# Batched attention on one Trainium2 core: the last K chunk of the first batch turned by a DMA transpose, and V released by another transpose

## The chip, the cores and the metric

The kernel runs on one core of one Trainium2 chip. The metric is the device time of one execution in microseconds (us), on the slowest core, which here is the only one. Engines are named as in the profile: PE (TensorE, matmuls), PEld (its weight loads), DVE (VectorE), ACT (ScalarE), POOL (GpSimd) and SP (SyncE). DMAs are issued from two places: POOL's queue (q0 in the profile, `software_dynamic`), which carries the loads that also cast from f32 to f16, and SP's queue (q1, `hardware_dynamic`), which carries plain copies, the output stores and the DMA transposes. Both run on the core's 16 DMA engines.

## The reference

Eight independent batches of softmax attention, 2048 rows of 512 each, in f32:

```python
batch, seq_len, d_model = 8, 2048, 512
scores = np.matmul(q, k.transpose(0, 2, 1)) / np.sqrt(d_k)
attn_weights = special.softmax(scores, axis=-1).astype(np.float32)
return np.matmul(attn_weights, v)
```

## The kernel before

**Work and tiles.** Everything on the matrix side is f16. For each batch K and Q are needed with the 512-long axis on the partitions, so they are transposed once; V is used as loaded. A batch has 16 blocks of 128 K rows, held as four chunks of four blocks (`kops[0..3]`), and 2048 queries, held as two spans of 1024 (`qraw[0]` and `qraw[1]`), each of two chunks. Chunks are called k0 to k3, q0 to q3 and v0 to v3 here: one chunk is 512 rows, 512 KB in f16. Q chunks 0 and 1 fill span one, 2 and 3 span two.

**How products are made.** Except for the first span of the first batch, both the scores and the product with V are computed by seven half-size products instead of eight (a Winograd form). This needs sums of blocks, made on DVE: `k_sums` (L181 to L184), `q_sums` (L191 to L194), `p_sums` (L327 to L330) and `v_sums` (L208 to L211). `Group.product` (matmuls at L278) makes scores of the span that is one ahead, `Pair.product` (matmuls at L373) multiplies exponentials with V. In the steady part these two kinds alternate on PE by a table of slots.

**The start of the program.** The first span of batch 0 has nothing ahead of it, so it is computed with plain matmuls (`plain_quarter` at L240, `plain_tile` at L227) while the data arrives. This stage fills about the first 41 us, and the change lies wholly in it. Its order is written out by hand, and every engine and queue follows its own instructions in that order:

- SP first loads q0 and k0 in rows of 128 (`load_first`), in f32; they are rounded and turned on PE.
- POOL then issues the cast loads, in this order: k1 (two halves), q1, k2, k3, q2, q3 (`load`, L118). k1 and k2 go to tiles of the pool `stage`; q1, k3, q2 and q3 go to four spare parts of `vraw[1]`, which no V needs yet. That is why the profile calls these `vh<-in_q_dram` and `vh<-in_k_dram`.
- k1, q1, k2 and k3 are turned on PE by `pe_transpose`: 16 matmuls against the identity (L153) into two PSUM tiles of the tag `px`, one copied out by DVE and one by ACT (L156). k3's stands ahead of the tile (10, 1); its first use is the tile (12, 0).
- q2 and q3 are turned by SP with `dma_transpose` (L143), SBUF to SBUF, one DMA each, in this order.
- POOL then makes a one-element copy, the gate (L576), from the last element of `qraw[1]`, which q3's transpose writes. The four V loads (`load_v`, L200) stand behind it on POOL, so they are not issued before q3's transpose has landed. Behind them, on the same queue, come the first loads of batch 1.
- When the plain tiles are done, PE starts the slot loop: the second span's scores, and from slot 5 on the first product with V (`FIRST` begins with `a1`), whose eight matmuls read v0 to v3 one after another.

The transposes on SP wait for their source to be loaded; SP executes nothing else between them and the first store, at 57 us.

Of the kernel before, what the change touches and what calls it, by code (L numbers as in the profile page):

```python
# [12 lines left out]
def kernel(  # L13
# [21 lines left out]
    nc = tc.nc  # L35
# [10 lines left out]
    ND = D // P  # L46
# [3 lines left out]
    NT = QH // P  # L50
    NQT = 2 * NSP
    NJ = NKB // 2
    CH = 4
# [22 lines left out]
    def bank(name):  # L76
        t = psum[name].tile([P, 512], F32, tag=name)
        return t
# [14 lines left out]
    qraw = [const.tile([P, 2 * NT, ND, P], F16, name=f"qraw{n}") for n in range(2)]  # L93
# [40 lines left out]
    def raw_of(what, b, c):  # L134

        if what == "k":
            return kops[c][0]
        return qraw[(b * NCH + c) // 2 % 2][:, c % 2 * CH:(c % 2 + 1) * CH]

    def dma_transpose(what, b, c):  # L140
        src = staged.pop((what, b, c))
        dst = raw_of(what, b, c)
        nc.sync.dma_start_transpose(  # L143
            out=dst[:, 0:CH].rearrange("p n c r -> p (n c) r"),
            in_=src[:].rearrange("p n d -> p (n d)"),
        )

    def transposed(what, c, n, w, copy):
        src = staged[what, 0, c]
        tr = psum["px"].tile([P, 2, ND, P], F16, tag="px", name="tr")  # L150
        for m in range(w):
            for dc in range(ND):
                nc.tensor.transpose(  # L153
                    tr[:, m, dc, :], src[:, n + m, dc * P:(dc + 1) * P], ident[:]
                )
        copy(out=raw_of(what, 0, c)[:, n:n + w], in_=tr[:, 0:w])  # L156
        if n + w == CH:
            staged.pop((what, 0, c))

    def pe_transpose(what, c, n0=0, n1=CH):  # L160
        for n in range(n0, n1, 2):
            transposed(what, c, n, 2, nc.scalar.copy if n else nc.vector.tensor_copy)
# [14 lines left out]
    def k_sums(c):  # L177
        a11, a12, a21, a22 = k_blocks(c)
        _, s1, s2, s4 = kops[c]
        return [  # L180
            lambda: add(s1[:], a21, a22),  # L181
            lambda: sub(a21, a11, a21),
            lambda: sub(s2[:], s1[:], a11),
            lambda: sub(s4[:], a12, s2[:]),  # L184
        ]

    def q_sums(sp):
        b11, b12, b21, b22 = q_blocks(sp)
        t1, t2, t4 = qsum
        return [  # L190
            lambda: sub(t1[:], b12, b11),  # L191
            lambda: sub(t2[:], b22, t1[:]),
            lambda: sub(b12, b22, b12),
            lambda: sub(t4[:], b21, t2[:]),  # L194
        ]
# [23 lines left out]
    def exp(out_, in_):  # L219
        nc.scalar.activation(out=out_, in_=in_, func=EXP, scale=inv_sqrt_d)  # L220

    def plain_tile(kb, half, name):

        st = bank(name)
        c, n = divmod(kb, CH)
        for dc in range(ND):
            nc.tensor.matmul(  # L227
                st[:], kops[c][0][:, n, dc, :], qraw[0][:, half * NT:(half + 1) * NT, dc, :],
                start=(dc == 0), stop=(dc == ND - 1),
            )  # L230
        left, right = pts[0]
        exp(right[:, kb // 2, kb % 2, :] if half else left[kb % 2][:, kb // 2, :], st[:])

    def plain_quarter(j, part):

        st = bank("qx")
        w = QH // 2
        for s in range(2):
            for dc in range(ND):
                nc.tensor.matmul(  # L240
                    st[:, s * w:(s + 1) * w], kops[0][0][:, 2 * j + s, dc, :],
                    qraw[0][:, 2 * part:2 * part + 2, dc, :],
                    start=(s == 0 and dc == 0), stop=(dc == ND - 1), skip_group_check=True,
                )
        for s in range(2):
            exp(pts[0][0][s][:, j, part * w:(part + 1) * w], st[:, s * w:(s + 1) * w])
# [67 lines left out]
    def p_sums(g, which, j0=0, j1=NJ):  # L314

        left, right = pts[g // 2]
        if (g, which) not in psums:
            psums[g, which] = [
                spool.tile([P, NJ, P], F16, tag=f"s{n}", name=f"s{n}") for n in (1, 2, 4)
            ]  # L320
        s1, s2, s4 = psums[g, which]
        cols = columns(g, which)
        js = slice(j0, j1)
        a11, a21 = left[0][:, js, cols], right[:, js, 0, cols]
        a12, a22 = left[1][:, js, cols], right[:, js, 1, cols]
        return [
            lambda: add(s1[:, js], a21, a22),  # L327
            lambda: sub(s2[:, js], s1[:, js], a11),
            lambda: sub(a21, a11, a21),
            lambda: sub(s4[:, js], a12, s2[:, js]),  # L330
        ]
# [198 lines left out]
    gate = const.tile([P, 1], F32)  # L530
# [39 lines left out]
    plain_quarter(1, 0)  # L570
    pe_transpose("k", 1, 0, 2)
    plain_quarter(1, 1)
    dma_transpose("q", 0, 2)
    dma_transpose("q", 0, 3)

    nc.gpsimd.tensor_copy(out=gate[:], in_=qraw[1][:, 2 * NT - 1, ND - 1, 0:1])  # L576
    for c in range(NCH):
        load_v(0, c)

# [3 lines left out]
    for n, (kb, half) in enumerate(rest):  # L583
        if (kb, half) == (5, 0):
            pe_transpose("k", 1, 2, 4)
        if (kb, half) == (6, 0):
            pe_transpose("q", 1)
        if (kb, half) in ((6, 1), (10, 1)):
            pe_transpose("k", kb // CH + 1)
        plain_tile(kb, half, "qz" if n % 3 == 2 else "qx")  # L590
        if half and kb % CH == 3:
            background.extend(k_sums(kb // CH))
        if (kb, half) == (12, 1):
            background.extend(p_sums(0, "a", 0, NE))
        if (kb, half) == (13, 1):
            background.extend(q_sums(1))
        if background:
            background.popleft()()
# [58 lines left out]
```

The softmax here doesn't subtract the row's maximum and nothing guards it: scores larger than these inputs give would overflow.

## Time and profile before

The median of five runs is 804.93 us (804.04 to 806.69). The profiled execution is one of the five.

| What | us |
|---|---|
| Median of the five runs | 804.93 |
| The profiled execution, its own time | 806.69 |
| Its span from the first to the last instruction | 804.9 |
| PE busy in the span | 795.5 (99%) |
| ACT busy | 571.2 (71%) |
| DVE busy | 547.9 (68%) |
| q0's packets, as a share of the 16 DMA engines' span | 42.8% |
| q1's packets, the same | 38.5% |

PE is busy nearly all the time and ran at the full granted clock (0.999). Of its waits in the first 70 us, one is long: 2.1 us at L373 for a V load. Waits of PE in this stretch, by what it waited for: the V load 2.1 us, the memset of the warm-up tile 1.2, the first rows' rounding 0.8, a copy of Q 0.6 in two pieces, q1's load 0.4, and a sum for V 0.3.

### The profile page before, as it was taken

What the parts mean: (1) busy time and instruction counts of PE and PEld (TensorE: products, weight loads), DVE (VectorE), ACT (ScalarE), POOL (GpSimd) and SP (SyncE); (2) the same over time, 40 slices, a digit from 0 to 9 for tenths busy, and PEclk for the clock granted to TensorE, in tenths of its full rate; (3) what the DMA queues carried; (4) which work ended last, traced back from release to release, by engine and by line L of the source; (5) the groups of instructions that cost most, each with busy time, mean ns of one, the idle gap of its engine ahead of it and who ended that gap; (6) DMA issues with size and microseconds to landing.
All of it is one profiled execution on the core that took longest, in us unless ns stands there. A gap on an engine that the chain in (4) does not pass through costs nothing.

```text
span 804.9 us, 14513 instructions
## 1 busy us (share of the span) xinstructions
PE 795.5 (99%) x5516; PEld 535.6 (67%) x5516; DVE 547.9 (68%) x1213; ACT 571.2 (71%) x1021; POOL 71.6 (9%) x104
## 2 busy tenths in 40 slices
PE   8989999999999999999999999999999999999998
PEld 4556666666666666666666666666666666666677
DVE  3475766857678676776757677686776857668564
ACT  5757777777777777777677677677777777776752
POOL 3301100011100111010100110001100011000000
PEclk9999999999999999999999999999999999999999
DMA  9999993699938999289993999949997499711112
GB/s 207 160 201 200 201 145 93 119 209 197 146 77 151 190 178 177 61 152 197 179 145 87 162 173 189 139 92 173 170 184 120 95 208 168 155 40 41 48 46 104
DMA packets 190229, 116.32 MB, mean 145 GB/s; under 512 B 124496, under 2 KB 172880, under 8 KB 190160
## 3 DMA queue, kind: packets, MB, share of 16 engines
q0 software_dynamic: 49648, 49.29, 42.8%
q1 hardware_dynamic: 140368, 66.08, 38.5%
q8 instruction: 43, 0.70, 0.4%
q14 instruction: 26, 0.21, 0.1%
q10 hardware_dynamic: 144, 0.03, 0.0%
HBM read 100.70 MB, written 33.55 MB: 167 GB/s over the span
## 4 chain that ended last, share of the span: by engine, by line
PE 94%; DMA 5%; POOL 1%; DVE 0%; issue 0%; ACT 0%; SPq 0%; POOLq 0%
PE t L373 49%; PE t L278 45%; DMA vh<-in_q_dram 2%; DMA vh<-in_v_dram 2%; DMA first<-in_q_dram 1%; DMA qraw<-vh 1%; POOL vh L200 0%; POOL vh L118 0%; ACT o L381 0%; DVE stage L132 0%; DVE qraw L156 0%; SPq L128 0%; POOL stage L118 0%; PE tr L153 0%; PE t L240 0%
## 5 line engine op out<-in xcount | busy, mean ns | idle before, releaser
L278 PE MATMUL t<-qraw,kraw 128*128 128x512 f16 x720 | 194.7, 379 | 0.0
L381 ACT ACTIVATE o<-t,r 128x256 f32<-128x256 f32 x256 | 121.3, 474 | 100.2 <-DVE r L401 67.3
L373 PEld LDWEIGHTS <-s 128*128 128x128 f16 x1536 | 150.3, 98 | 57.0
L220 ACT ACTIVATE left<-t 128x512 f16<-128x512 f32 (+1 forms) x260 | 154.6, 596 | 41.7 <-PE t L278 37.1
L384 DVE SCALAR_TENSOR_TENSOR o<-t,r,o 128x256 f32<-128x256 f32 x192 | 92.4, 482 | 108.7 <-PE t L373 52.1
L278 PEld LDWEIGHTS <-kraw 128*128 128x128 f16 x960 | 93.9, 98 | 62.2
L373 PE MATMUL t<-vh,left 128*128 128x256 f16 x1024 | 133.0, 273 | 2.1 <-DMA vh<-in_v_dram 2.1
L278 PE MATMUL t<-qs,ks 128*128 128x512 f16 x480 | 133.1, 379 | 0.3 <-DVE vt L208 0.3
L373 PE MATMUL t<-vt,s 128*128 128x257 f16 (+1 forms) x1024 | 133.0, 273 | 0.0
L220 ACT ACTIVATE right<-cz 128x1024 f16<-128x1024 f32 x120 | 127.3, 1061 | 1.1 <-DVE cz L298 1.1
L373 PEld LDWEIGHTS <-left 128*128 128x128 f16 x1024 | 100.2, 98 | 39.6 <-issue 2.5
L373 PEld LDWEIGHTS <-right 128*128 128x128 f16 x1024 | 100.2, 98 | 38.4 <-issue 0.4
L292 ACT COPY cz<-t 128x512 f32<-128x512 f32 x120 | 70.2, 585 | 72.7 <-PE t L278 72.3
L298 DVE TENSOR_TENSOR cz<-t,cz 128x512 f32<-128x512 f32 x120 | 82.4, 687 | 51.7 <-PE t L278 51.7
L301 DVE TENSOR_TENSOR cz<-t,cz 128x512 f32<-128x512 f32 x120 | 82.7, 689 | 37.4 <-PE t L278 37.4
L278 PEld LDWEIGHTS <-ks 128*128 128x128 f16 x720 | 70.4, 98 | 47.4 <-issue 0.8
L278 PE MATMUL t<-qs,kraw 128*128 128x512 f16 x240 | 71.4, 379 | 0.0
L278 PE MATMUL t<-qraw,ks 128*128 128x512 f16 x240 | 71.4, 379 | 0.0
L288 ACT COPY t<-t 128x512 f32<-128x512 f32 x120 | 68.4, 570 | 3.3 <-PE t L278 0.6
L295 ACT COPY cz<-t 128x512 f32<-128x512 f32 x120 | 69.8, 582 | 0.2 <-PE t L278 0.2
L373 PE MATMUL t<-vt,right 128*128 128x256 f16 x512 | 67.2, 273 | 0.0
L373 PE MATMUL t<-vh,s 128*128 128x257 f16 x512 | 66.7, 273 | 0.0
(54 smaller groups left out, 577.2 us busy)
## 6 DMA issues: line engine op xcount, KB each, us to landing
out_dram<-o SPq DMA_DIRECT2D x127, 256.0 KB, 3.1
vh<-in_v_dram POOLq DMA_DIRECT2D x32, 512.0 KB, 9.8
stage<-in_k_dram POOLq DMA_DIRECT2D x29, 512.0 KB, 7.0
stage<-in_q_dram POOLq DMA_DIRECT2D x28, 512.0 KB, 8.0
vh<-in_q_dram POOLq DMA_DIRECT2D x3, 512.0 KB, 13.2
first<-in_q_dram SPq DMA_DIRECT2D x2, 256.0 KB, 3.7
first<-in_k_dram SPq DMA_DIRECT2D x2, 256.0 KB, 3.9
cz<-in_q_dram SPq DMA_DIRECT2D x2, 256.0 KB, 5.0
```

The source lines that it names most:

```text
L220: nc.scalar.activation(out=out_, in_=in_, func=EXP, scale=inv_sqrt_d)
L278: nc.tensor.matmul(dst[:], lhs[:, j, dc, :], rhs[:, :, dc, :], start=(n in (1, 5) and dc == 0), stop=(dc == 1), skip_group_check=True,)
L288: nc.scalar.copy(out=self.y[:], in_=self.x[:])
L292: nc.scalar.copy(out=self.cz[:, 1, :], in_=self.z[:])
L295: nc.scalar.copy(out=self.cz[:, 0, :], in_=self.x[:])
L298: nc.vector.tensor_add(self.cz[:, 1, :], self.x[:], self.cz[:, 1, :])
L301: nc.vector.tensor_add(self.cz[:, 0, :], self.z[:], self.cz[:, 0, :])
L373: nc.tensor.matmul(dst[:, 0:width], lhs(j), rhs(j), start=(first and j == 0), stop=(j == NJ - 1), skip_group_check=True,)
L381: nc.scalar.activation(out=out_, in_=src, func=COPY, scale=r[:])
L384: nc.vector.scalar_tensor_tensor(out=out_, in0=src, scalar=r[:], in1=out_, op0=MULT, op1=ADD)
```

## The change

k3 is no longer turned on PE. A DMA transpose for it is put on SP's queue, ahead of those of q2 and q3. The gate in front of the V loads reads the last element of the first half of `qraw[1]`, which q2's transpose writes, instead of the last of the second half, which q3's writes.

```diff
     plain_quarter(1, 0)
     pe_transpose("k", 1, 0, 2)
     plain_quarter(1, 1)
+    dma_transpose("k", 0, 3)
     dma_transpose("q", 0, 2)
     dma_transpose("q", 0, 3)
 
-    nc.gpsimd.tensor_copy(out=gate[:], in_=qraw[1][:, 2 * NT - 1, ND - 1, 0:1])
+    nc.gpsimd.tensor_copy(out=gate[:], in_=qraw[1][:, NT - 1, ND - 1, 0:1])
     for c in range(NCH):
         load_v(0, c)
...
             pe_transpose("k", 1, 2, 4)
         if (kb, half) == (6, 0):
             pe_transpose("q", 1)
-        if (kb, half) in ((6, 1), (10, 1)):
-            pe_transpose("k", kb // CH + 1)
+        if (kb, half) == (6, 1):
+            pe_transpose("k", 2)
         plain_tile(kb, half, "qz" if n % 3 == 2 else "qx")
```

On the engines: PE loses 16 transposes (L153), DVE and ACT lose one copy each (L156), SP gains one DMA transpose in front of the two it has. POOL keeps the same instructions in the same order; only what the gate reads differs. After the start of batch 0 no engine's instructions change.

## The prediction

> **What bounds the kernel now.** I read the page's chain shares first, then the chain in order of time over the first 52 us, then PE's and SP's own timelines there, then the DMA engines stretch by stretch.
>
> ```profile
> PE 94%; DMA 5%; POOL 1%; DVE 0%; issue 0%; ACT 0%; SPq 0%; POOLq 0%
> ```
>
> The end is set by PE for 94% of the span. The 5% of DMA can only be at the start, and the chain shows where (start, us, what):
>
> ```profile
> 12.01 15.09 DMA vh<-in_q_dram
> ...
> 27.11 4.38 DMA qraw<-vh
> ...
> 31.63 0.18 POOL gate L576
> ...
> 32.08 1.31 POOL vh L200 x2
> ...
> 34.28 12.68 DMA vh<-in_v_dram
> ...
> 47.00 0.38 PE t L373 x2
> ```
>
> From 12 to 47 us the end hangs on transfers: q3's load, q3's transpose (landed at 31.49), the gate, the V issues, v3's landing at 46.96. From 47 us on it is PE without a gap. So what counts is when v3 lands, or, if that comes early enough, when PE is ready for it. PE's timeline:
>
> ```profile
> 31.24 1.06 PE L153 MATMUL tr<-ident,vh 128*128 128x128 f16 x16
> ...
> 43.91 0.96 PE L373 MATMUL t<-vh,left 128*128 128x256 f16 x6
> 47.00 0.38 PE L373 MATMUL t<-vh,left 128*128 128x256 f16 x2 [2.13 <-DMA vh<-in_v_dram]
> ```
>
> k3's transposes cost PE 32.13 - 31.24 = 0.89 us until the next tile starts, 1.06 with the overlap; I take 1.0. PE then waits 2.13 us for v3. SP's queue (start, time SP spends on the issue):
>
> ```profile
> 24.53 5.21 SPq L143 DMA_TRANSPOSE qraw<-vh  x2
> 49.63 5.43 SPq L143 DMA_TRANSPOSE qraw<-stage  x1
> ...
> 155.06 4.97 SPq L143 DMA_TRANSPOSE qraw<-stage  x1
> 160.13 3.66 SPq L143 DMA_TRANSPOSE kraw<-stage  x1
> ```
>
> The issue of one transpose holds SP 2.63 and 1.41 us for q2 and q3 (the min and max of this group), but about 5 us where loads keep the DMA engines full. Last, the DMA engines (stretch, length, busy us of PE, PEld, DVE, ACT, POOL, clock, DMA share, GB/s):
>
> ```profile
> 22.00:25.00 3.00, 3.00 (x25) 1.70 (x24) 0.81 (x3) 2.20 (x4) 0.00 (x0) 1.00 1.23 204
> 25.00:27.10 2.10, 2.10 (x16) 1.08 (x14) 1.72 (x5) 1.61 (x3) 0.00 (x0) 1.00 1.05 139
> 27.10:31.20 4.10, 4.10 (x20) 1.86 (x19) 0.78 (x3) 2.99 (x5) 0.00 (x0) 1.00 1.10 216
> 31.20:35.00 3.80, 3.80 (x31) 2.21 (x30) 1.53 (x4) 2.78 (x5) 3.10 (x5) 1.00 0.36 36
> 35.00:47.00 12.00, 9.56 (x46) 4.32 (x45) 9.27 (x23) 6.89 (x12) 3.06 (x6) 1.00 1.20 190
> ```
>
> Loads alone run full at 204 GB/s; the change-over to transposes is poorer (139); transposes alone make 216; then there is a hole of 3.8 us (36 GB/s) between q3's transpose and V's full rate; then V. The hole is free room.
>
> [...] Where loads and the transpose of 49.63 meet (54 to 56 us), the packets are about equal in number, and a load's is 1 KB, a transpose's 256 bytes:
>
> ```profile
> q0 software_dynamic: 307, 0.31, 92.1%
> q1 hardware_dynamic: 299, 0.08, 29.4%
> ```
>
> Loads alone moved 0.41 MB in 2 us (51 to 53), so they fall to 76%, and a transpose gets some 40 GB/s. [...] 216 is measured here and is what I use.
>
> **The change part by part.**
>
> *PE.* 16 transposes go: -1.0 us at 31 us. PE comes to v3's matmuls at 44.87 - 1.0 = 43.9 instead of 44.87. If v3 still lands at 46.96 this only makes the wait 3.1 us instead of 2.1. DVE and ACT lose a 0.69 and a 1.01 us copy, off the path: nothing. Should v3 be on time, the floor is -1.0 - 2.1 = -3.1 us.
>
> *k3's transpose on SP.* k3 was issued on POOL at 10.54 and landed after 11.4 us, at 21.9. So the transpose issues at 21.9, where the DMA engines are full of q2 and q3 until 27.1. Its use moves to 31.1 us, so it has 9.2 us. The transpose of 49.63 took 10.5 us to land, but under loads that went on to 58.2 us (the last issued at 37.25, landing after 20.9). That of 155.06 took 9.0, until 164.1. Here the loads end at about 27, and q2's transpose before landed at 24.53 + 4.7 = 29.2. I take k3 landing by 30: no wait. If it is late by a microsecond or two, the 3.1 us of slack ahead of v3 hide it.
>
> *q2's transpose and the gate.* q2's transpose follows on SP when k3's issue is over, so it inherits the place that q3's had. Two pairs in the trace bound it. Before's pair q2, q3 took from 24.53 to 31.49, 7.0 us for both. The pair issued under loads at 155.06 and 160.13 landed second at 160.13 + 5.7 = 165.8, 10.8 us. From 21.9 that gives 28.9 to 32.7 for q2 against 31.49 for q3 before: the gate moves by -2.6 to +1.2 us. The low end has a reason against it: the engines have no free room before 25 us, so k3's packets before then only push q2's and q3's loads back. Only the poor change-over from 25 to 27.1 can be filled, worth 2.1 x (1 - 139/204) = 0.7 us. I take -0.6.
>
> *q3's transpose beside V.* It now runs after the gate: 0.52 MB / 216 GB/s = 2.4 us of the engines. If it follows q2's packets without a gap it is over about 2 us after the gate, and V's first packets were seen some 2 us after it (33.5 against 31.63) and V's full rate 3.4 us after it. So it mostly fits in the hole. The bounds are 0 and the whole 2.4 us. I take +0.6, a quarter of it, because V's first packets are then shared. q3's next reader is `q_sums` on DVE at 37.63, three microseconds later than I expect it landed; behind it on DVE stand the sums for k3, and behind those PE's products, all of which run into the V wait anyhow.
>
> *Queues.* On SP nothing but the first store (57.17) is behind the three transposes. On POOL, V and then batch 1's loads move with the gate; their transposes start at 49.63 and are first read at L191 at 87.39 us, so a microsecond is hidden. Nothing after the start is reordered.
>
> Sum: v3 lands at 46.96 - 0.6 + 0.6 = 46.96, PE's gain becomes waiting: 0.0 us. The profiled execution's own time is 806.69, of which its span is 804.9 and 1.8 lie around it; it is 1.76 above the median of the runs. As the sum is zero I set the forecast at the median, **804.9 us**. What can be told from no change is about 0.2%, 1.6 us.
>
> **The rivals.**
>
> *No change* (the forecast, 58%): 803.4 to 806.5. V's landing moves by less than 1.6 us either way. For it: the DMA engines are full from 10 to 31 us, and a third transpose adds work there that roughly eats the hole it fills.
>
> *V pays for q3's transpose* (slower, 26%): 807.3. If q3's issue is held on SP as that of 49.63 was (5.4 us), its packets are still queued when V comes to full rate. From then they take turns with V's, V drops to 76%, and v3 lands up to 2.4 us later, 804.93 + 2.4 = 807.3. It decides from the point where most of q3's 2048 packets are left 3.4 us after the gate; then the gate itself being late (+1.2) would add to it. For it: SP's 5 us issues, and that a transpose trickles as long as loads run. Against it: the three are queued before V is, and two queued transposes ran 216 GB/s without a gap.
>
> *V comes early* (faster, 16%): 802.3. If k3's packets pass between the loads and q2's pair time stays 7.0 us, the gate opens 2.6 us earlier, v3 lands near 44.4, still after PE's 43.9, and all of it is gained: 804.93 - 2.6. Against it: no free DMA room before 25 us. At the most it is -3.1.
>
> That the DMA transpose doesn't do its part is no rival: k3 has nine microseconds.
>
> **How the numbers follow.** 58, 26 and 16 in a hundred, and the chances of same, slower and faster are these, since each case lies on one side of 0.2%. The range goes from 802.4 to 807.5: it holds the forecast's own and a little over half of each of the other cases, and leaves out gains over 2.5 us and losses over 2.6.
>
> **What would show it.** In the profile after: no L153 at 31 us; k3's transpose issued near 21.9 with an issue of 2.6 to 5.4 us; the gate between 29 and 32.7; v3's landing within 1.6 of 46.96; and a PE wait at L373 of about 3 us. I am wrong if that wait is under 1.5 us (V came early), if v3 lands after 48.6 with transpose packets still among V's, or if PE waits for k3 near 31 us for so long that it sets the end.

## The result, and the profile after

The changed kernel takes 809.45 us (median of 26 runs, 805.88 to 816.0) against 805.09 us for the kernel before (47 runs, 803.69 to 810.82). The ratio is 1.0054, 95% interval 1.0042 to 1.0066: slower by 4.4 us. The profiled execution took 810.99 us, with a span of 808.8; it is 1.5 us above its median.

The chain shares of the page hardly differ from before:

```profile
PE 93%; DMA 5%; POOL 0%; DVE 0%; issue 0%; ACT 0%; SPq 0%; ACTq 0%; POOLq 0%
```

The chain in order of time (start, us, what) at the start, and a second stretch of it that the kernel before does not have:

```profile
11.40 14.42 DMA vh<-in_q_dram
...
25.84 6.40 DMA qraw<-vh
...
32.37 0.18 POOL gate L577
...
35.02 12.71 DMA vh<-in_v_dram
...
47.77 0.59 PE t L373 x2
...
70.00 0.18 SPq L143
...
70.28 10.71 DMA out_dram<-o
...
81.08 0.48 ACT o L381
```

The gate follows q2's transpose now, and comes 0.74 us later than before (32.37 against 31.63); v3 lands at 47.73 instead of 46.96. That is a fifth of the 3.9 us by which the two spans differ. The rest is in PE's own timeline (the bracket is the idle time ahead and what ended it):

```profile
43.66 0.60 PE L373 MATMUL t<-vh,left 128*128 128x256 f16 x4
45.23 0.38 PE L373 MATMUL t<-vh,left 128*128 128x256 f16 x2 [0.98 <-DMA vh<-in_v_dram]
47.77 0.59 PE L373 MATMUL t<-vh,left 128*128 128x256 f16 x2 [2.16 <-DMA vh<-in_v_dram]
48.16 1.91 PE L278 MATMUL t<-qraw,kraw 128*128 128x512 f16 x4
49.86 1.66 PE L373 MATMUL t<-vt,s 128*128 128x257 f16 x8
...
81.60 1.03 PE L373 MATMUL t<-vt,s 128*128 128x256 f16 x8 [1.18 <-ACT o L381]
```

The two groups after v3 in the kernel before:

```profile
47.22 1.02 PE L278 MATMUL t<-qraw,kraw 128*128 128x512 f16 x4
48.08 1.04 PE L373 MATMUL t<-vt,s 128*128 128x257 f16 x8
```

Two things are to be seen. After v3 the next four matmuls take 1.91 us and the eight after them 1.66; the same groups took 1.02 and 1.04 before. And at 81.60 PE waits 1.18 us for ACT, a wait that the kernel before doesn't have. The table of PE by stretches (length, busy time, granted clock, DMA share, GB/s) tells what the first is:

```profile
44.00:46.00 2.00, 0.63 (x5) 1.00 1.25 209
46.00:48.00 2.00, 0.23 (x2) 0.93 1.24 205
48.00:50.00 2.00, 2.00 (x7) 0.50 1.24 205
50.00:52.00 2.00, 2.00 (x12) 0.72 1.25 207
52.00:54.00 2.00, 2.00 (x15) 1.00 1.24 206
```

PE was busy 0.86 us of 4, and then the clock was granted at 0.50. The lost time is 2 x 0.07 + 2 x 0.50 + 2 x 0.28 = 1.7 us, that is 3.4 us at half clock.

In this trace the clock was full from 6.75 us, where its record begins, to 47.71 (40.96 us), half for 3.413, and full again for 757.76: 12, 1 and 222 times 3.413 us. In the kernel before it was full from 4.69 to 803.41 us (798.72), 234 times 3.413. Both are as if the clock changed only at the edges of windows of 3.413 us, counted from where its record begins. These windows around the wait for V, first of the changed kernel, then of the kernel before (the columns as above):

```profile
44.29:47.70 3.41, 0.38 (x2) 1.00 1.24 206
47.70:51.12 3.42, 3.35 (x12) 0.50 1.25 208
...
42.23:45.65 3.42, 2.33 (x12) 1.00 1.24 205
45.65:49.06 3.41, 2.06 (x15) 1.00 1.24 207
```

In the changed kernel one window holds nearly the whole wait, and the next one is granted half the clock. In the kernel before, the wait of 2.13 us falls across an edge (45.65), and the clock stays at 1.00. Of all the windows of these two traces, two were followed by half clock within the span: the one with 0.38 us of PE's work, and one with 1.19 at the end of the kernel before (799.99 to 803.41). Every other one that has its next window in the span held 2.06 us or more, and the clock was full after it. In after_o6 the half clock began near 45.48, and PE had been busy about 1.45 of the 3.41 us ahead of it (an estimate from its table by stretches of 2 us, where the clock of 44 to 46 us is 0.87, and from its PE timeline). And in k3_from_k2 one wait of PE was 3.6 us long, while the mean clock of that execution was 0.999. So by these traces it counts where a wait falls, and not only how long it is.

The second thing is SP's queue. The first batch-1 transposes and the stores behind them:

```profile
60.09 2.19 SPq L143 DMA_TRANSPOSE qraw<-stage  x1
62.38 7.80 SPq L143 DMA_TRANSPOSE kraw<-stage  x1
70.28 6.66 SPq L391 DMA_DIRECT2D out_dram<-o  x3
```

The transpose of 62.38 holds SP 7.80 us and lands after 17.0 us (5.31 and 7.3 before). The same transpose before, and the time to landing (the last figure) before and after:

```profile
61.70 5.31 SPq L143 DMA_TRANSPOSE kraw<-stage  x1
kraw<-stage SPq DMA_TRANSPOSE x1, 7.3
...
kraw<-stage SPq DMA_TRANSPOSE x1, 17.0
```

The store behind it is issued at 70.28 and lands after 10.7 us; until then ACT waits with the next result, and PE waits for ACT. So the profile's 3.9 us are 0.8 from v3, 1.6 from the half clock (1.91 + 1.66 - 1.02 - 1.04 = 1.5 from these two groups, the rest from the two matmuls ahead of them), which leaves 1.5 around the 1.18 us wait, since PE runs without a gap from there to the end. These three are what the experiments take apart.

Each execution comes with its mean granted clock, so the half clock can be counted without a profile: 3.4 us at half clock lower the mean by 1.7/809 = 0.002. Half clock at the very end, where PE has no work left, can take up to 0.001 more: in the profile of before the clock was 0.50 for the last 1.49 us, 0.75/805 = 0.0009, and the mean 0.999. At 0.998 or less stood 18 of 27 executions of the changed kernel, and 26 of 166 of the kernel before, as it ran beside the experiments. Seven of the 18 stood at 0.996 or less, so by this estimate their clock fell more than once. The 18 have a median of 810.8 us and the nine others 807.6: the half clock is not the whole loss.

### The profile page after: what moved, and what is told of

It reads as the page before. It is cut to its first block, busy times and chain, and to the rows that moved or that the text cites. A ratio compares the mean times of both kernels' runs of the same rounds, so it can differ in the third digit from the quotient of the medians.

```text
span 808.8 us, 14480 instructions
## 1 busy us (share of the span) xinstructions
PE 797.6 (99%) x5500; PEld 535.9 (66%) x5500; DVE 547.6 (68%) x1212; ACT 570.1 (70%) x1020; POOL 71.5 (9%) x104
## 4 chain that ended last, share of the span: by engine, by line
PE 93%; DMA 5%; POOL 0%; DVE 0%; issue 0%; ACT 0%; SPq 0%; ACTq 0%; POOLq 0%
PE t L373 48%; PE t L278 44%; DMA vh<-in_q_dram 2%; DMA vh<-in_v_dram 2%; DMA out_dram<-o 1%; DMA qraw<-vh 1%; PE t L542 1%; POOL vh L200 0%; ACT o L381 0%; PE tr L153 0%; DVE qraw L156 0%; POOL stage L118 0%; POOL vh L118 0%; DVE stage L132 0%; PE t L240 0%
## 6 DMA issues: line engine op xcount, KB each, us to landing
vh<-in_v_dram POOLq DMA_DIRECT2D x32, 512.0 KB, 10.7
```

## The experiments

Ratios are against the kernel before, run beside each on the same chip. Its median was 805.15 us beside k_only, gate_only, after_warm and after_o6; 805.57 beside k3_from_k2, after_warm_o6, before_warm and k3_second; 805.67 beside k3_from_k2_warm, before_o6 and gate_o6; and 804.72 beside before_late.

**k_only: the added transpose with the old gate.**

```diff
-    nc.gpsimd.tensor_copy(out=gate[:], in_=qraw[1][:, NT - 1, ND - 1, 0:1])
+    nc.gpsimd.tensor_copy(out=gate[:], in_=qraw[1][:, 2 * NT - 1, ND - 1, 0:1])
```

> The changed kernel with the gate back on q3's transpose. Theory A (the added transpose is what costs): V is released by the third transpose, which landed near 34.9 us in the profile of the changed kernel instead of 32.2, so v3 lands near 50.3, PE waits over 5 us and falls to half clock: about 812 us. Theory B (the early gate is what costs, since V then meets q3's transpose): without that meeting the loss goes, 806 us or less.

Measured: 810.66 us, ratio 1.0063 (1.0039 to 1.0086), from six executions. All six executions had a mean clock of 0.998 or less. In the profile the gate opens at 34.31, v3 lands at 48.80, and PE waits 2.04 and 2.15 us. The early gate isn't what costs: without it the kernel is no faster. The loss is smaller than A said, since q3's transpose landed at 34.19, less late than I had taken.

**gate_only: the gate moved alone.**

```diff
-    nc.gpsimd.tensor_copy(out=gate[:], in_=qraw[1][:, 2 * NT - 1, ND - 1, 0:1])
+    nc.gpsimd.tensor_copy(out=gate[:], in_=qraw[1][:, NT - 1, ND - 1, 0:1])
```

> The kernel before with only the gate moved to q2's transpose; k3 stays on PE. Theory A: q2's transpose lands near 29.2, the gate opens 2.3 us earlier, v3 lands near 44.7, PE hardly waits, no half clock: about 803 us. Theory B: V meets q3's transpose on the DMA engines and lands no earlier or later than 46.96: 805 to 808 us.

Measured: 804.0 us, ratio 0.9982 (0.9971 to 0.9993), a gain of 1.2 us. The gate and PE's first product with V, from POOL's and PE's timelines:

```profile
29.48 0.18 POOL L576 CAST gate<-qraw 128x1 f32<-128x1 f16 x1 [16.26 <-DMA qraw<-vh]
```

```profile
44.30 1.03 PE L373 MATMUL t<-vh,left 128*128 128x256 f16 x8
```

The gate opens 2.15 us earlier than in the profile of before, all eight matmuls run without a wait, and none of 22 executions had a mean clock under 0.999. The gain is less than the 2.1 us that the profile of before promised: once V is on time PE's own work sets the end, and the profiled execution of before, 1.8 us above its median, may have waited longer than most: before_o6, which has the same opening, waited 1.12 us for V in its profile.

**after_warm: the changed kernel with PE kept busy in the wait.**

```diff
             if slot in todo:
+                if g == 0 and todo[slot] == "a1":
+                    keep = bank("py")
+                    for _ in range(10):
+                        nc.tensor.matmul(keep[:], warm[:, 0:P], warm[:], start=True, stop=True)
                 pv(g, todo[slot])
```

> The changed kernel with ten matmuls on zeros into an unused PSUM tile ahead of PE's first product with V (2.2 us of the 3.1 us that PE waits there; the output doesn't change). Theory A (the long wait sets PE to half clock for one window of 3.4 us, which costs 1.6 us): no stretch of clock 0.5 after 47 us, about 807.8 us. Theory B (the clock is a coincidence or costs nothing): as the changed kernel, 809.4 us.

Measured: 806.44 us, ratio 1.0007 (0.9993 to 1.0020). PE's timeline:

```profile
42.41 2.32 PE L628 MATMUL t<-warm 128*128 128x512 f16 x10
44.56 0.82 PE L373 MATMUL t<-vh,left 128*128 128x256 f16 x6
46.22 0.38 PE L373 MATMUL t<-vh,left 128*128 128x256 f16 x2 [0.84 <-DMA vh<-in_v_dram]
46.44 1.02 PE L278 MATMUL t<-qraw,kraw 128*128 128x512 f16 x4
47.30 1.04 PE L373 MATMUL t<-vt,s 128*128 128x257 f16 x8
```

V is as late as it was, PE does nothing useful meanwhile, and still 3.0 us of the 4.4 are gone: the groups after v3 are back at 1.02 and 1.04 us, and none of the 14 executions had a mean clock under 0.999. That is more than the half clock's own 1.6; in this profile no wait for ACT is left either.

**after_o6: the changed kernel with six output tiles.**

```diff
-    opool = ctx.enter_context(tc.tile_pool(name="opool", bufs=4))
+    opool = ctx.enter_context(tc.tile_pool(name="opool", bufs=6))
```

> The changed kernel with six instead of four output tiles. Theory A (PE's second wait, 1.2 us at 80 us, is for an output tile whose store stood on SP behind a transpose that loads held up): that wait is gone, about 808.2 us. Theory B (the wait is hidden or moves on): 809.4 us.

Measured: 807.57 us, ratio 1.0025 (1.0014 to 1.0036), 1.9 us less than the changed kernel. In its profile the half clock is there, the transpose ahead of the stores again holds SP for 8.76 us, and PE has no wait for ACT. So the store wait is real and costs 1.9 us in the median. With the tiles out of the way the half clock can be read off by itself: the 16 executions at 0.998 or less have a median near 807.6, the six others 805.9 (two of the six took over 808).

**k3_from_k2: PE's transposes of k3 left out, nothing added on the DMA engines.**

```diff
-        if (kb, half) in ((6, 1), (10, 1)):
-            pe_transpose("k", kb // CH + 1)
+        if (kb, half) == (6, 1):
+            pe_transpose("k", 2)
+        if (kb, half) == (10, 1):
+            nc.vector.tensor_copy(out=kops[3][0][:, 0:2], in_=kops[2][0][:, 0:2])
+            nc.scalar.copy(out=kops[3][0][:, 2:4], in_=kops[2][0][:, 2:4])
+            staged.pop(("k", 0, 3))
```

Batch 0 is computed without its fourth K chunk here: the third stands in its place.

> The kernel before, but the PE transposes of k3 are left out and nothing is done in their place on the DMA engines: DVE and ACT copy the transposed k2 into k3's tile (so the last quarter of K in batch 0 is a repeat of the third). Theory A (a longer PE wait alone does it): V lands as before, PE comes 1.0 us earlier, waits 3.1 us and falls to half clock for 3.4 us: 806.7 us, up to 808 if the store wait follows. Theory B (the loss is the DMA transpose's traffic): 805.1 us, as before.

Measured: 811.2 us, ratio 1.0057 (1.0038 to 1.0076). This is the decisive run: less work on PE, the same DMAs as before, and the whole loss is there, 3 us more than A allowed. It doesn't need the added transpose. 13 of 17 executions had a mean clock of 0.998 or less, and took 807.9 to 813.5 (eight of them at 0.996 or less); of the other four, three took 805.3 to 805.6. The fourth is the profiled one (812.24), which shows that the store wait can come without the half clock. Its wait for V, 2.22 us, is no longer than the 2.13 of before, so this trace doesn't show the longer wait of theory A; that is inferred from the clocks of the 13, none of which was profiled. Who PE waited for there (us in total, times, longest):

```profile
PE t L373 <- ACT o L381: 4.4, 2, 3.6
PE t L373 <- DMA vh<-in_v_dram: 2.2, 1, 2.2
PE t L278 <- DVE cz L301: 1.5, 1, 1.5
```

**k3_from_k2_warm: the same with the ten matmuls of after_warm.**

> The kernel before without a transpose of k3 (k3's tile is a copy of k2's, so the last quarter of K in batch 0 is a repeat) and with the ten matmuls on zeros ahead of the first product with V. Theory A (the loss of 5.6 us without these matmuls comes from PE's long wait, the store waits included): near 805.5 us, and a mean clock of 0.999 or 1.0 in every execution. Theory B (the store waits come from PE's earlier arrival itself): still over 808 us.

Measured: 805.56 us, ratio 0.9989 (0.9972 to 1.0005), every mean clock 0.999 or 1.0. Filling PE's wait takes away all 5.6 us, the store waits included. With the run before it, this puts the loss on PE's idling ahead of v3: PE's work is as short as there, and costs nothing once the wait is filled.

**after_warm_o6: both remedies on the changed kernel.**

> The changed kernel with both the ten matmuls that keep PE busy and six output tiles. Theory A (the store wait follows from PE's late phase after the half clock): as with the ten matmuls alone, 806.4 us. Theory B (the two losses are independent): 1.9 us less than with the ten matmuls alone, 804.5 us.

Measured: 806.06 us, ratio 1.0006 (0.9996 to 1.0016), as A said. Once PE doesn't idle, two more tiles gain 0.4 us by the medians and 0.1 by the ratios, not told from nothing, instead of 1.9: the store wait goes with the idle time.

**before_warm and before_o6: the same remedies on the kernel before.**

> The kernel before with the ten matmuls on zeros ahead of the first product with V (2.2 us, about the length of PE's wait). Theory A (2.1 us of waiting doesn't trip the clock in most executions): no gain, 805.1 to 805.5 us, with fewer of the executions above 806.5. Theory B (it trips often, which the profile missed): 804 us or less.

> The kernel before with six output tiles. Theory A (the wait for an output tile is a consequence of the change): no gain, 805.2 us. Theory B (it is there before too): as in the changed kernel 1.9 us less, 803.5 us.

Measured: 805.73 us, ratio 1.0005 (0.9999 to 1.0012), and 805.4 us, ratio 0.9999 (0.9991 to 1.0007). Neither gains: the median execution of before has neither loss. Of before_warm's 22 executions 20 lie between 805.17 and 806.59, where before reaches from 803.95 to 809.6. The best executions are a microsecond worse with the ten matmuls, and the worst ones 1.5 better.

**k3_second: k3's transpose between q2's and q3's.**

```diff
-    dma_transpose("k", 0, 3)
     dma_transpose("q", 0, 2)
+    dma_transpose("k", 0, 3)
     dma_transpose("q", 0, 3)
```

> The changed kernel with k3's transpose between those of q2 and q3, the gate on q2's. Theory A (what counts is how early V is released and that PE doesn't wait long): the gate opens near 29.5 as with the gate moved alone, k3 lands near 31.5, so PE waits about 0.5 us for k3 and 1 us for v3, no half clock: 803.5 to 804.5 us. Theory B (a third transpose costs wherever it stands, by its traffic beside V): 807 us or more.

Measured: 812.94 us, ratio 1.0101 (1.0085 to 1.0117), from six executions, of which the profiled one (809.01) is the fastest. A missed. B's number holds, but it was V's loads that held up a transpose, and q3's, not k3's. The gate opened early (28.66), so V's loads were issued together with q3's transpose (from 29.11 and 29.07 on). That transpose then landed only after 14.25 us, and the longest of PE's waits is for the sum of Q that needs it:

```profile
29.07 14.25 DMA qraw<-vh
```

```profile
PE t L278 <- DVE qs L191: 3.7, 1, 3.7
```

The half clock followed here too (mean clocks 0.994 to 0.998). This is the prediction's slower rival turned round: the transpose pays for V, not V for the transpose.

**before_late: before_warm with more matmuls, to see if being late brings the store wait.**

> The kernel before with eighteen instead of ten matmuls on zeros ahead of the first product with V: PE stays busy, so at full clock, but goes on about 1.7 us later, as late as a window of half clock would leave it. Theory A (store waits follow because PE's slots then stand about 1.7 us later against the loads): 805.7 + 1.7 = 807.4 from the matmuls, and store waits on top of it, 809 us or more. Theory B (being late is not what brings the store waits): 807.4 us.

```diff
-                    for _ in range(10):
+                    for _ in range(18):
```

Measured: 807.46 us, ratio 1.0024 (1.0014 to 1.0034), all mean clocks 0.999 or 1.0. B: PE goes on as late as a half-clock window would leave it, and nothing comes on top. So the store wait goes together with PE's idling, and being late alone doesn't bring it, as far as the kernel before can show. How the two are linked stays open.

**gate_o6: the gate moved alone, with six output tiles.**

> The gate moved alone, with six output tiles. Theory A (after the V wait is gone PE sets the end, only rare executions wait for a store): 803.8 to 804.0 us. Theory B (store waits still cost in most executions): 803 us or less.

Measured: 803.9 us, ratio 0.9979 (0.9969 to 0.9988), the slowest of 16 executions at 804.62. It is faster than both kernels, by 1.8 us and 5.5 us. Of this gate_only brings nearly all.

## Why the prediction was wrong

It said 804.9 us with 802.4 to 807.5; 809.45 is outside. By its steps:

- *PE comes 1.0 us earlier and only waits longer: "PE's gain becomes waiting: 0.0 us".* This is the step that failed. The wait was sized rightly (3.1 us; 0.98 + 2.16 measured, and 2.73 in after_o6), but it was costed at its length, as if PE went on at full speed after it. It put PE to half clock for 3.4 us, in 18 of 27 executions by their mean clocks, and store waits went with it; the sum has nothing for either. k3_from_k2 shows that the shorter PE work is enough for the whole loss, and k3_from_k2_warm and after_warm that filling the wait takes it away (all of it in the first, 3.0 of 4.4 us in the second).
- *v3's landing unchanged, at 46.96.* Right within the 1.6 us that were allowed. It was 47.73 in the profile of the changed kernel, whose first loads came late, and 46.18, 46.21 and 45.96 in after_warm, after_o6 and after_warm_o6, which have the same opening. The 46.96 itself is one execution: before_o6, with the opening of before, has 45.08.
- *The gate between 28.9 and 32.7, k3 landing by 30.* The gate opened at 32.37 there and at 30.83 to 30.89 in the next two; k3's transpose landed at 23.30 + 7.1 = 30.4, and PE didn't wait for it. It had more time than the 9.2 us of the prediction, since PE's transposes of k3 stood three tiles ahead of its first use.
- *0.7 us of poor change-over could be filled.* No. From loads to transposes the DMA engines moved less (stretch, length, busy us of PE, PEld, DVE, ACT, POOL, clock, DMA share, GB/s, of the changed kernel): 83 GB/s for 3.5 us, where before had 139 for 2.1. In this execution the engines nearly stood still from 27 to 28 us (0 to 20 GB/s). Over the 4.8 us around the end of the loads (2.1 before it, 2.7 after) before moved 198 GB/s and this execution 118. After_warm, after_o6 and after_warm_o6, which have the same opening, had the gate at 30.89, 30.83 and 30.49, where before_o6, with the opening of before, had it at 30.65: no 0.7 us was gained there either.

```profile
25.00:28.50 3.50, 3.50 (x30) 2.08 (x29) 2.49 (x7) 2.71 (x4) 0.00 (x0) 1.00 1.17 83
28.50:32.20 3.70, 3.70 (x19) 1.67 (x18) 0.38 (x2) 2.51 (x5) 0.00 (x0) 1.00 1.08 233
32.20:35.00 2.80, 2.80 (x15) 1.26 (x13) 0.76 (x2) 2.00 (x4) 2.36 (x4) 1.00 1.07 191
```

- *q3's transpose fits in the hole ahead of V.* Right for the most part: from 32.2 to 35 us the engines moved 191 GB/s, where before left them a hole, and V's last load takes 12.71 us from its issue, as before (12.68). Before_o6 and k3_from_k2 needed only 11.77 and 12.01 for it, so a cost of up to 0.9 us, near the 0.6 that was charged, isn't excluded. The slower rival, in which V pays 2.4 us for q3, did not happen.
- *"Nothing after the start is reordered", so nothing there costs.* Wrong in effect: the store wait at 80 us is 33 us past the change, in instructions that the diff doesn't touch. SP's next instruction behind the three transposes is also not the first store but batch 1's first transpose (49.63 before, 50.47 after), and the store wait hangs on batch 1's transposes.

The prediction leaves out what a wait does to PE's clock. In the changed kernel the clock was granted at 0.50 for 3.41 us, from 47.71 on, as the wait ended. It took no single gap of that length: gaps of 0.98 and 2.16 us with 0.38 us of work between them were enough, and in after_o6 gaps of 0.57 and 2.16, with about 1.45 us of work in the 3.41 us ahead (the estimate above). In 26 of 166 executions of before the mean clock was 0.998 or less, so by the estimate from the mean clocks it fell there too, most likely behind before's own wait, which was 2.13 us where it was profiled, at full clock.

What stays open is why transposes and stores of batch 1 are held up after PE has idled. In the two profiles where PE waits for ACT, POOL began to issue two loads 4.3 and 3.3 us before SP was through with the issue of k0's transpose (63.09 against 67.34 in k3_from_k2, 66.92 against 70.18 in the changed kernel). Before had them 0.4 us apart, and after_o6 and k_only, whose profiles have no such wait, 1.5 and 2.0. This is a reading, and no run tested it.

## What to carry to other kernels

Work saved on PE that turns into waiting is not free here: add the waits that fall close together, and if they can leave PE with as little work in 3.41 us as here (0.38 us in the changed kernel and, as estimated, about 1.45 in after_o6; 2.06 in before did no harm), count another 1.7 us for the clock, which is what it cost in the changed kernel. A profiled execution that escaped can have been lucky in where its wait fell (before: 0.999 in the profile, 0.998 or less in 26 of 166 executions), so look at the mean clocks of many. Where the wait can't be avoided, matmuls on zeros can fill it (before_warm: 0.05%, not told from nothing). Better is to move the release of what PE waits for, alone: here one index of the gate gave 1.2 us, and the transpose that came with it took that and 4 us more.

## What the runs showed of the hardware

- Half clock lasted 3.41 us in the changed kernel, and 3.40 in k_only and after_o6 by their tables of stretches of 2 us (clocks 0.74, 0.50, 0.91 and 0.87, 0.50, 0.78), and cost 1.6 to 1.7 us in the changed kernel. PE had been busy 0.38 us of the 3.41 us ahead there, and by estimate from these tables and PE's timelines about 0.50 in k_only and 1.45 in after_o6. In k3_second the wait ahead was 3.73 us, and the four matmuls behind it took 1.89 us, where those at half clock in the changed kernel took 1.91.
- The stretches of one clock ahead of the last change were whole multiples of 3.413 us: 12, 1 and 222 in the changed kernel, 234 in the kernel before. A wait of 2.13 us across the edge of such a window left 2.33 and 2.06 us of work on its two sides in the profile of before, and the clock stayed at 1.00. A wait of 3.6 us in k3_from_k2 stood in an execution with a mean clock of 0.999.
- While the transposes queued ahead of V's loads ran, the DMA engines moved 191 to 233 GB/s (the changed kernel, 28.5 to 35 us). A transpose issued just as such a stream of loads began took 14.25 us to land (k3_second), and the one at 62 us in the changed kernel, among loads, took 17.0.
- A microsecond of work taken off PE ahead of a wait raised the median by 5.6 us, with not one DMA changed (k3_from_k2), and ten matmuls on zeros in the wait took that back (k3_from_k2_warm).
